# New states of eight streams from doubled rows: two products instead of three, no mask, and the weighting of the doubled rows behind that of the plain rows

## The chip, the cores and the metric

The kernel runs on one core of one Trainium2 chip. The metric is the device time of one execution in microseconds; the number that counts is the median over several runs. The engines are named as the profile names them: PE (TensorE; PEld is its weight load), DVE (VectorE), ACT (ScalarE), POOL (GpSimd) and SP (SyncE, which only issues DMAs here).

## What is computed

One layer of a streaming encoder for 256 prompt rows and, beside them, 16 new rows for each of 8 running streams: 384 rows in all. The layer is a projection, a pooling branch, a state space (SSD) branch, gates, an output product, and an MLP. The change lies in the SSD branch, at the end of this step of the reference:

```python
def step(h, inp):
    xc, dtc, Bc, Cc = inp
    cum = jnp.cumsum(dtc * A, axis=1)
    ...
    y = jnp.einsum('btsgr,bsgrp->btgrp', cb[..., None] * decay, xdt)
    y = y + jnp.einsum('btgn,bgrpn->btgrp', Cc, h) * jnp.exp(cum)[..., None]
    last = cum[:, -1]
    w_end = jnp.exp(last[:, None] - cum)
    h = h * jnp.exp(last)[..., None, None] + jnp.einsum('bsgn,bsgr,bsgrp->bgrpn', Bc, w_end, xdt)
    return h, y
```

The sum over `s` in the last line runs over the 16 rows of one stream for each of the 8 streams `b`: the state that a stream hands on is its old one, decayed, plus a product of the rows `B` with the rows `x`, weighted by `w_end` and `dt`. There are 8 groups `g`, each with 8 heads of 64 channels, and 128 state columns `n`. All of it is fp32.

## The kernel before

**Products.** PE has no fast fp32 product, so the kernel splits each operand into a high part (a cast to the type fp32r, on ACT) and a low part (the operand less its high part, on DVE) and adds three products: high by high, high by low, low by high. For the weights this is `wsplit` (L70 the cast `wh`, L71 the subtraction `wl`), and `mm3` (L101, L102, L103) issues the three; only L103 reads `wl`. A weight matrix comes in half units of 512 KB: a half is fetched by SP's queue, split by ACT and DVE, and read by 24 matmuls. Three halves lie in SBUF at once.

**The SSD stage** runs from about 425 to 1165 us. Its loop goes over the 8 groups. A group projects ten units: x, B, x, C, x, x, all six with a convolution (`cbuf`, `cstate`, `cacc`, `xs`), and four of z (`zproj`, each of two halves). A group's heads form two pairs, `D.p[0]` and `D.p[1]`. Between the projections stand "lumps", short stretches of matmuls that need what the other engines have prepared:

- the middle of a group (behind its fifth unit): for the pair `p[1]` of the group before, the prompt's state (`t_pp`), its outputs (`t_yT`, `t_Y`) and the streams' new states (`t_su`); and for this group's `p[0]` the contribution of the old states (`t_yi`);
- the end of a group: the same for this group's `p[0]`, with `t_yi` of `p[1]`. The last group's `p[1]` follows behind the loop.

**The streams' new states.** `t_su` (L803 on) stands 16 times in the program. It uses PE as four row tiles of 32 rows. The 128 stream rows (16 for each of 8 streams) lie on the 128 partitions, so that one row tile `q` holds the rows of two streams, `2q` and `2q+1`. To get two sums out of one tile, the rows `B` stand twice in `Bm`, once with the second stream's rows put to zero and once with the first's (a multiplication by a mask from `vec`, on ACT, L728). For each of the two and each tile three products are added, as above: 2 × 3 × 4 = 24 matmuls. Four `hs` adds on DVE (L818) then put them onto the decayed states, two streams each, and a DMA stores these.

**What is prepared for it.** `turned` (L622) turns a 128x384 tile of x or B to rows: DVE transposes in blocks (`xb`, L627), POOL stores the blocks to a scratch in DRAM with four DMAs (L632) and fetches them in the right place (L638) as three blocks of 128 rows: two of the prompt, the third the stream rows. `xside` (L758) multiplies the rows by the weights in `tok` on DVE, into `xdt` for the outputs and into `xT` in place for the states. `hside` (L769) splits `xT` into `xhl` on ACT and DVE. `bside` (L721) does so for B and makes `Bm`.

**The order around it.** The kernel is written in one order and a scheduler sets each engine's own; `behind` holds an instruction behind another, `later` and `dve_later` behind the last split of a weight half. Each engine works in its order: an instruction that waits holds all that is behind it. In the middle of a group, `xside` and `hside` of `p[0]` follow on DVE and ACT right behind the lump, together with the convolution of the sixth unit and the splits of the z weights; at the start of a group `p[1]` of the group before is prepared.

## Time and profile before

| | |
|---|---|
| median of 3 runs | 2642.29 us (2642.28 to 2642.95) |
| the profiled execution | 2643.02 us |
| its span | 2641.2 us |
| mean granted clock of PE | 0.999 |
| POOL, share of the span | 9% |
| PE instructions in the profile | 16317 |
| `hs` adds (DVE, L818) | 64, of 0.673 to 0.680 us |
| split `wh_z` (ACT, L70) / `wl_z` (DVE, L71), mean | 1.04 / 1.22 us |

How to read it: the span is that of the profiled execution. "Busy" is the time in which an engine worked. A row of a timeline gives the start in us from the span's start, the duration, the engine, the line of the kernel, the operation, output and inputs, shapes and count, and in square brackets how long the engine stood idle before it and what ended that. A row with "x2" joins neighbours of one kind. On DVE and ACT an instruction's record begins some 0.07 to 0.15 us before the one ahead of it ends, so that starts give the pitch better than durations. In a row of the view by tile the three numbers are the shortest, median and longest duration in ns, then the first and the last start in us.

### The profile page before, as it was taken

The page shows a single profiled execution, that of the slowest core. Times are in us where ns is not written, and L with a number is a line of the kernel's source. Part 1 is how long each engine was busy: PE and PEld are TensorE (multiplying, and loading weights), DVE is VectorE, ACT ScalarE, POOL GpSimd, SP SyncE. Part 2 cuts the span into 40 slices and gives each one's busy share as a digit, 9 for nine tenths or more (in the row PEclk, how much of TensorE's full clock was granted, in tenths as well). Part 3 has the DMA queues.
Part 4 walks back from the last instruction along what each step waited for, and adds up shares of the span by engine and source line. Part 5 has one row for each costly group of instructions (what it writes and reads, how often), then busy time and mean ns, then how long its engine had stood idle before and what let it go on. Part 6 is the DMA issues. An engine that isn't in the chain of part 4 may idle for free.

```text
span 2641.2 us, 40716 instructions
## 1 busy us (share of the span) xinstructions
PE 2631.5 (100%) x16317; PEld 2530.6 (96%) x16317; DVE 1544.6 (58%) x2192; ACT 1161.5 (44%) x1781; POOL 242.4 (9%) x382
## 2 busy tenths in 40 slices
PE   9999999999999999999999999999999999999998
PEld 9999999999999999999999989999999999989897
DVE  6685335788888888867444336534444444444446
ACT  6443324657565656545333336433333333323233
POOL 0000002123222322211000000000000000000000
PEclk9999999999999999999999999999999999999999
DMA  7444446566676666657555544444444444444443
GB/s 274 148 135 154 148 147 222 190 202 227 211 233 201 219 225 230 220 189 261 163 166 160 196 148 132 144 136 136 136 136 136 136 136 135 136 134 136 136 135 131
DMA packets 130318, 451.50 MB, mean 171 GB/s; under 512 B 17936, under 2 KB 24912, under 8 KB 125136
## 3 DMA queue, kind: packets, MB, share of 16 engines
q1 hardware_dynamic: 103552, 361.44, 42.1%
q0 software_dynamic: 19520, 72.64, 7.8%
q10 hardware_dynamic: 7056, 14.81, 1.9%
q8 instruction: 128, 2.10, 0.3%
q14 instruction: 62, 0.51, 0.1%
HBM read 404.49 MB, written 44.34 MB: 170 GB/s over the span
## 4 chain that ended last, share of the span: by engine, by line
PE 99%; ACT 0%; DVE 0%; DMA 0%; DVEq 0%; issue 0%
PE pj_up L101 6%; PE pj_up L103 6%; PE pj_up L102 6%; PE wd L156 6%; PE wd L154 6%; PE wd L155 6%; PE pj_x L101 5%; PE pj_x L102 5%; PE pj_x L103 5%; PE pj_z L103 3%; PE pj_z L101 3%; PE pj_sp L103 3%; PE pj_sp L102 3%; PE pj_sp L101 3%; PE pj_z L102 3%; PE pj_gb L101 2%
## 5 line engine op out<-in xcount | busy, mean ns | idle before, releaser
L101 PE MATMUL pj_up<-x1h,wh_up 128*128 128x384 f32 (+1 forms) x1024 | 333.7, 326 | 0.0
L102 PE MATMUL pj_up<-x1l,wh_up 128*128 128x384 f32 (+1 forms) x1024 | 333.4, 326 | 0.0
L103 PE MATMUL pj_up<-x1h,wl_up 128*128 128x384 f32 (+1 forms) x1024 | 333.4, 326 | 0.0
L71 DVE TENSOR_TENSOR wl_wd<-w_wd,wh_wd 128x1024 fp32r<-128x1024 f32 x126 | 154.3, 1225 | 240.5 <-ACT wh_wd L70 240.5
L154 PE MATMUL wd<-wh_wd,hh 128*128 128x512 f32 x756 | 286.5, 379 | 0.0
L155 PE MATMUL wd<-wl_wd,hh 128*128 128x512 f32 x756 | 286.5, 379 | 0.0
L156 PE MATMUL wd<-wh_wd,hl 128*128 128x512 f32 x756 | 286.5, 379 | 0.0
L70 ACT ACTIVATE wh_wd<-w_wd 128x1024 fp32r<-128x1024 f32 x126 | 133.1, 1057 | 321.8 <-PE wd L156 261.4
L70 ACT ACTIVATE wh_up<-w_up 128x1024 fp32r<-128x1024 f32 x126 | 133.1, 1057 | 292.2 <-PE pj_up L102 231.8
L71 DVE TENSOR_TENSOR wl_up<-w_up,wh_up 128x1024 fp32r<-128x1024 f32 x126 | 154.3, 1225 | 178.3 <-ACT wh_up L70 178.2
L101 PE MATMUL pj_x<-xgh,wh_x 128*128 128x384 f32 x768 | 251.9, 328 | 0.0
L102 PE MATMUL pj_x<-xgl,wh_x 128*128 128x384 f32 x768 | 250.4, 326 | 0.0
L103 PE MATMUL pj_x<-xgh,wl_x 128*128 128x384 f32 x768 | 250.4, 326 | 0.0
L102 PEld LDWEIGHTS pj_up<-x1l,wh_up 128*128 128x128 f32 x1024 | 193.6, 189 | 0.2
L101 PEld LDWEIGHTS pj_up<-x1h,wh_up 128*128 128x128 f32 x1024 | 193.6, 189 | 0.2
L103 PEld LDWEIGHTS pj_up<-x1h,wl_up 128*128 128x128 f32 x1024 | 193.6, 189 | 0.0
L103 PE MATMUL pj_z<-xgh,wl_z 128*128 128x384 f32 x512 | 167.3, 327 | 0.0
L101 PE MATMUL pj_z<-xgh,wh_z 128*128 128x384 f32 x512 | 166.9, 326 | 0.0
L102 PE MATMUL pj_z<-xgl,wh_z 128*128 128x384 f32 x512 | 166.9, 326 | 0.0
L101 PE MATMUL pj_sp<-abh,wh_sp 128*128 128x384 f32 x512 | 166.9, 326 | 0.0
L102 PE MATMUL pj_sp<-abl,wh_sp 128*128 128x384 f32 x512 | 166.9, 326 | 0.0
L103 PE MATMUL pj_sp<-abh,wl_sp 128*128 128x384 f32 x512 | 166.9, 326 | 0.0
(334 smaller groups left out, 6183.5 us busy)
## 6 DMA issues: line engine op xcount, KB each, us to landing
w_up<-w_up SPq DMA_DIRECT2D x128, 512.0 KB, 3.5
w_wd<-w_down SPq DMA_DIRECT2D x128, 512.0 KB, 3.5
w_x<-w_in SPq DMA_DIRECT2D x96, 512.0 KB, 4.1
w_z<-w_in SPq DMA_DIRECT2D x64, 512.0 KB, 4.2
w_sp<-w_ssd SPq DMA_DIRECT2D x64, 512.0 KB, 3.5
w_ga<-w_ga SPq DMA_DIRECT2D x32, 512.0 KB, 3.5
w_pp<-w_pp SPq DMA_DIRECT2D x32, 512.0 KB, 3.4
hs<-ssm POOLq DMA_DIRECT2D x16, 1024.0 KB, 8.0
```

The costliest lines, as they stand in the source:

```text
L70: cut[0] = s.activation(h, w, AF.Copy)
L71: cut[1] = v.tensor_tensor(l, w, h.bitcast(F32), ALU.subtract)
L101: te.matmul(out, wh, xh, start=first, stop=False, **how)
L102: te.matmul(out, wh, xl, start=False, stop=False, **how)
L103: return te.matmul(out, wl, xh, start=False, stop=last, **how)
L154: te.matmul(out, mh, vh, start=k == 0 and b != held, stop=False, skip_group_check=b == held)
L155: te.matmul(out, mh, vl, start=False, stop=False, skip_group_check=b == held)
L156: last[0] = te.matmul(out, ml, vh, start=False, stop=k == nk - 1, skip_group_check=b == held)
```

## The change

The two streams of a row tile are told apart by position and no longer by a mask. Besides the plain rows, each turned tile is fetched a second time with every stream row twice: `doubled` lets partition 2t and partition 2t+1 hold the same row `t` of the 64 rows of half `l` (streams 0 to 3, and 4 to 7). A row tile of 32 partitions then holds the 16 rows of one stream, each twice. On the even partitions of `xd` stands the high part with a minus, on the odd ones the low part; `Bd` is B times −1 on the even and +1 on the odd partitions, once its high part and once its low part. One product over 32 partitions so adds (−high)(−high B) and (low)(high B) in one go, and a second does the same with the low part of B: two products for each half `l` and tile `q`, that is 2 × 2 × 4 = 16 matmuls in place of 24. The tile `su[q]` now belongs to the streams `q` and `q + 4`, so the `hs` adds take those.

What goes: `Bm` and its two ACT casts a group, the third block of `xhl`, `Bhl`, `Bt` and of the product on `xT`. What comes: for each turned tile two more POOL DMAs of 64 KB, at the stage's start a scratch store and two loads for `tokd` (the weights of the doubled rows); for each pair a product `xD` on DVE, a cast `xd` on ACT and a subtraction `xd` on DVE; for each group a cast `Bd` on ACT and a subtraction `Bd` on DVE. The two parity columns of `vec` change their values. The product on `xD` is held behind the last product of `xside`, the cast `xd` behind the cast of `xhl`.

```diff
@@ -210,6 +210,7 @@
     ma_scr = [dram.tile([P, T], F32, name=f"ma_scr{i}") for i in range(KD)]
     gb_scr = [dram.tile([P, T], F32, name=f"gb_scr{i}") for i in range(KD)]
     t_scr = [dram.tile([T, P], F32, name=f"t_scr{i}") for i in range(40)]
+    d_scr = dram.tile([P, NH], F32, name="d_scr")
     cum_scr = dram.tile([NH, T], F32, name="cum_scr")
     dec_scr = dram.tile([NH, NB], F32, name="dec_scr")
 
@@ -619,7 +620,15 @@
         def conv(ui, c, tag, nb, hook=None):
             return taps(conv_in(ui, c, hook), c, tag, nb)
 
-        def turned(src, i, o):
+        def doubled(o, src):
+            for q in range(2):
+                gp.dma_start(o[q::2], src.rearrange("(l t) n -> t l n", l=2))
+
+        tokd = pd.tile([P, 2, NH], F32, name="tokd", bufs=1)
+        gp.dma_start(d_scr, tok[:, 8])
+        doubled(tokd, d_scr)
+
+        def turned(src, i, o, od):
             xb, scr = [], t_scr[i]
 
             def turn():
@@ -635,13 +644,20 @@
                     )
 
             wait = [lambda: None] if i < 32 else []
-            steps.append(wait + [turn, spread, lambda: gp.dma_start(o, scr.rearrange("(b t) n -> t b n", b=3))])
+            nb = o.shape[1]
+
+            def fetch():
+                gp.dma_start(o, scr[: nb * P].rearrange("(b t) n -> t b n", b=nb))
+                doubled(od, scr[TP:])
+
+            steps.append(wait + [turn, spread, fetch])
 
         def xturned(D, g, j):
             S = D.p[j // 2]
             if j % 2 == 0:
                 S.xT = pd.tile([P, 2, 3, P], F32, tag="xT", name=f"xT{S.nm}", bufs=1)
-            turned(D.xs[j], g * 4 + j, S.xT[:, j % 2])
+                S.xD = pd.tile([P, 2, 2, P], F32, tag="xD", name=f"xD{S.nm}", bufs=1)
+            turned(D.xs[j], g * 4 + j, S.xT[:, j % 2], S.xD[:, :, j % 2])
 
         def lump(fn):
             with behind(last[0]):
@@ -719,17 +735,15 @@
             return i
 
         def bside(D):
-            D.Bhl = pd.tile([P, 2, 3, P], F32R, tag="Bhl", name=f"Bhl{D.g}", bufs=1)
+            D.Bhl = pd.tile([P, 2, 2, P], F32R, tag="Bhl", name=f"Bhl{D.g}", bufs=1)
+            D.Bd = pd.tile([P, 2, 2, P], F32R, tag="Bd", name=f"Bd{D.g}", bufs=1)
+            sign = vec[:, V_PAR + 1 : V_PAR + 2]
             with dve_later():
                 s.activation(D.Bhl[:, 0], D.Bt, AF.Copy)
                 v.tensor_tensor(D.Bhl[:, 1], D.Bt, D.Bhl[:, 0].bitcast(F32), ALU.subtract)
-            D.Bm = pd.tile([P, 2, 2, P], F32R, tag="Bm", name=f"Bm{D.g}", bufs=1)
-            for h in range(2):
-                s.activation(
-                    D.Bm[:, h],
-                    D.Bhl[:, :, 2, :].bitcast(F32),
-                    AF.Copy,
-                    scale=vec[:, V_PAR + h : V_PAR + h + 1],
+                s.activation(D.Bd[:, 0], D.BD, AF.Copy, scale=sign)
+                v.scalar_tensor_tensor(
+                    out=D.Bd[:, 1], in0=D.BD, scalar=sign, in1=D.Bd[:, 0].bitcast(F32), op0=ALU.mult, op1=ALU.subtract
                 )
 
         def cside(D):
@@ -758,18 +772,34 @@
             S.xdt = pd.tile([P, 2, 3, P], F32, tag="xdt", name=f"xdt{S.nm}", bufs=1)
             for q in range(2):
                 tv = S.xT[:, q].rearrange("p b (h q) -> p b h q", h=2)
-                for o, i in ((S.xdt, 3), (S.xT, 6)):
-                    v.tensor_tensor(
-                        o[:, q].rearrange("p b (h q) -> p b h q", h=2),
-                        tv,
-                        tok[:, i : i + 3, S.h0 + q * 2 : S.h0 + q * 2 + 2].unsqueeze(3).to_broadcast([P, 3, 2, 64]),
+                for o, i, nb in ((S.xdt, 3, 3), (S.xT, 6, 2)):
+                    done = v.tensor_tensor(
+                        o[:, q, :nb].rearrange("p b (h q) -> p b h q", h=2),
+                        tv[:, :nb],
+                        tok[:, i : i + nb, S.h0 + q * 2 : S.h0 + q * 2 + 2].unsqueeze(3).to_broadcast([P, nb, 2, 64]),
                         ALU.mult,
                     )
+            xD = S.xD.rearrange("p l j (h q) -> p l (j h) q", h=2)
+            with behind(done):
+                v.tensor_tensor(
+                    xD, xD, tokd[:, :, S.h0 : S.h0 + 4].unsqueeze(3).to_broadcast([P, 2, 4, 64]), ALU.mult
+                )
 
         def hside(S):
-            S.xhl = pd.tile([P, 2, 2, 3, P], F32R, tag="xhl", name=f"xhl{S.nm}", bufs=1)
-            S.split = s.activation(S.xhl[:, 0], S.xT, AF.Copy)
-            v.tensor_tensor(S.xhl[:, 1], S.xT, S.xhl[:, 0].bitcast(F32), ALU.subtract)
+            S.xhl = pd.tile([P, 2, 2, 2, P], F32R, tag="xhl", name=f"xhl{S.nm}", bufs=1)
+            S.split = s.activation(S.xhl[:, 0], S.xT[:, :, :2], AF.Copy)
+            v.tensor_tensor(S.xhl[:, 1], S.xT[:, :, :2], S.xhl[:, 0].bitcast(F32), ALU.subtract)
+            S.xd = pd.tile([P, 2, 2, P], F32R, tag="xd", name=f"xd{S.nm}", bufs=1)
+            with behind(S.split):
+                s.activation(S.xd, S.xD, AF.Copy)
+            v.scalar_tensor_tensor(
+                out=S.xd,
+                in0=S.xD,
+                scalar=vec[:, V_PAR : V_PAR + 1],
+                in1=S.xd.bitcast(F32),
+                op0=ALU.mult,
+                op1=ALU.subtract,
+            )
 
         def eside(S, q):
             if q == 0:
@@ -802,19 +832,19 @@
         def state(S):
             def t_su():
                 su = [sstile(f"su{S.nm}_{q}") for q in range(4)]
-                for h in range(2):
-                    for n, (bl, xl) in enumerate(((0, 0), (0, 1), (1, 0))):
+                for l in range(2):
+                    for part in range(2):
                         for q in range(4):
                             t = slice(q * 32, q * 32 + 32)
                             i = te.matmul(
-                                pairs(su[q][:, h * 256 : h * 256 + 256]),
-                                S.D.Bm[t, h, bl, :],
-                                S.xhl[t, xl, :, 2, :].rearrange("p j n -> p n j"),
-                                start=n == 0,
-                                stop=n == 2,
+                                pairs(su[q][:, l * 256 : l * 256 + 256]),
+                                S.D.Bd[t, part, l],
+                                S.xd[t, l].rearrange("p j n -> p n j"),
+                                start=part == 0,
+                                stop=part == 1,
                             )
                 for q in range(4):
-                    hr = S.hs[:, 2 * q : 2 * q + 2].rearrange("p h (a n) -> p h a n", a=2)
+                    hr = S.hs[:, q::4].rearrange("p h (a n) -> p h a n", a=2)
                     v.tensor_tensor(hr, hr, su[q].rearrange("p (h n a) -> p h a n", h=2, a=2), ALU.add)
                 return i
 
@@ -929,8 +959,9 @@
                 xturned(D, g, 0)
                 eside(prev.p[1], 0)
             D.BT = conv(u0 + 1, 32 + g, "BT", 2, None if g else first_behind)
-            D.Bt = pd.tile([P, 3, P], F32, tag="Bt", name=f"Bt{g}", bufs=1)
-            turned(D.BT, 32 + g, D.Bt)
+            D.Bt = pd.tile([P, 2, P], F32, tag="Bt", name=f"Bt{g}", bufs=1)
+            D.BD = pd.tile([P, 2, P], F32, tag="BD", name=f"BD{g}", bufs=1)
+            turned(D.BT, 32 + g, D.Bt, D.BD)
             if g:
                 eside(prev.p[1], 1)
                 expside(prev.p[1])
@@ -1458,8 +1489,8 @@
     vec[:, V_DSK:V_DTB] = chan(np.repeat(a["d_skip"][0], 64))
     vec[:NH, V_DTB] = a["dt_bias"][0]
     vec[:NH, V_ALOG] = a["a_log"][0]
-    for h in range(2):
-        vec[:, V_PAR + h] = (np.arange(P) // TS_) % 2 == h
+    vec[:, V_PAR] = np.arange(P) % 2
+    vec[:, V_PAR + 1] = 2.0 * (np.arange(P) % 2) - 1.0
     d = {
         "cst": _consts(np),
         "vec": vec,
```

The change also lets the scheduler come to another order. DVE in the middle of one group (the others but the first read alike), behind the lump: `hs` are the old pair's states, `xdt`, `xT`, `xD` the new pair's rows, `wl_z` the low halves of the z weights. Before:

```order
L762 TENSOR_TENSOR xdt_0_7615<-xT_0_7174,tok 128x384 x2
L818 TENSOR_TENSOR hs_1_6843<-hs_1_6843,su_1_0_7562 128x512
...
L762 TENSOR_TENSOR xT_0_7174<-xT_0_7174,tok 128x384 x2
L627 STREAM_TRANSPOSE xb_7685<-xs_7613 128x384
L772 TENSOR_TENSOR xhl_0_7620<-xT_0_7174,xhl_0_7620 128x768
L71 TENSOR_TENSOR wl_z_0_1_7658<-w_z_0_1_7655,wh_z_0_1_7657 128x1024
L593 TENSOR_TENSOR cbuf_4141<-pj_x_7624,rstd 128x12x16 x2
L71 TENSOR_TENSOR wl_z_1_0_7712<-w_z_1_0_7709,wh_z_1_0_7711 128x1024
```

With the change, from the same point on:

```order
L848 TENSOR_TENSOR hs_1_6875<-hs_1_6875,su_1_0_7598 128x2x256
...
L776 TENSOR_TENSOR xdt_0_7643<-xT_0_7202,tok 128x384 x2
L776 TENSOR_TENSOR xT_0_7202<-xT_0_7202,tok 128x256 x2
L784 TENSOR_TENSOR xD_0_7203<-xD_0_7203,tokd 128x512
L636 STREAM_TRANSPOSE xb_7718<-xs_7641 128x384
L791 TENSOR_TENSOR xhl_0_7649<-xT_0_7202,xhl_0_7649 128x512
L795 SCALAR_TENSOR_TENSOR xd_0_7652<-xD_0_7203,vec,xd_0_7652 128x512
L71 TENSOR_TENSOR wl_z_0_1_7691<-w_z_0_1_7688,wh_z_0_1_7690 128x1024
L594 TENSOR_TENSOR cbuf_4142<-pj_x_7657,rstd 128x12x16 x2
L613 SCALAR_TENSOR_TENSOR cacc_7725<-cbuf_4142,vec,cacc_7725 128x384 x2
L71 TENSOR_TENSOR wl_z_1_0_7745<-w_z_1_0_7742,wh_z_1_0_7744 128x1024
```

The four `hs` adds have moved ahead of `xdt`, two instructions on `xD` and `xd` stand between, and two `cacc` steps have moved ahead of the second `wl_z` of the piece (the third half of the z weights).

ACT at the same place, from the cast of `xhl` on. Before:

```order
L771 ACTIVATE xhl_0_7620<-xT_0_7174 128x768
L70 ACTIVATE wh_z_0_1_7657<-w_z_0_1_7655 128x1024
L789 ACT_TABLE_LOAD
L789 ACTIVATE E_0_7699<-E_0_7699 128x2048
L70 ACTIVATE wh_z_1_0_7711<-w_z_1_0_7709 128x1024
L601 COPY cbuf_4141<-cbuf_4141 128x15x3
L602 COPY cstate<-cbuf_4141 128x27
L610 ACTIVATE cacc_7692<-cbuf_4141,vec 128x384
L661 DMA cbc_1_1_7790<-cum_scr 128x768
L197 ACTIVATE nh_g_7936<-ssum_7084 128x384
L70 ACTIVATE wh_z_1_1_7745<-w_z_1_1_7743 128x1024
```

With the change:

```order
L790 ACTIVATE xhl_0_7649<-xT_0_7202 128x512
L794 ACTIVATE xd_0_7652<-xD_0_7203 128x512
L70 ACTIVATE wh_z_0_1_7690<-w_z_0_1_7688 128x1024
L819 ACT_TABLE_LOAD
L819 ACTIVATE E_0_7732<-E_0_7732 128x2048
L602 COPY cbuf_4142<-cbuf_4142 128x15x3
L603 COPY cstate<-cbuf_4142 128x27
L611 ACTIVATE cacc_7725<-cbuf_4142,vec 128x384
L70 ACTIVATE wh_z_1_0_7744<-w_z_1_0_7742 128x1024
L677 DMA cbc_1_1_7825<-cum_scr 128x768
L70 ACTIVATE wh_z_1_1_7778<-w_z_1_1_7776 128x1024
```

The cast `xd` has come behind that of `xhl`; the split of the third z half now follows the three convolution steps instead of leading them, and `nh_g` has left the piece.

POOL between two turned tiles of a group and the lump. Before:

```order
L632 DMA t_scr_141<-xb_5373 32x12x32 x4
L638 DMA xT_0_5124<-t_scr_141 128x3x128
L847 TENSOR_TENSOR ssum_5034<-ssum_5034,ysq_2_5550 128x384
L847 TENSOR_TENSOR ssum_5034<-ssum_5034,ysq_3_5555 128x384
L822 DMA new_ssm_s<-hs_1_4821 128x2048
```

With the change:

```order
L641 DMA t_scr_141<-xb_5397 32x12x32 x4
L650 DMA xT_0_5142<-t_scr_141 128x3x128
L625 DMA xD_0_5143<-t_scr_141 64x2x128 x2
L877 TENSOR_TENSOR ssum_5048<-ssum_5048,ysq_2_5568 128x384
L877 TENSOR_TENSOR ssum_5048<-ssum_5048,ysq_3_5573 128x384
L852 DMA new_ssm_s<-hs_1_4843 128x2048
```

Each fetch is followed by the two doubled loads; nothing else changes place on POOL here.

## The prediction

> **What bounds the kernel now.** I read the page first, for the engine that sets the end, then the view of the waits of TensorE.
>
> ```profile
> PE 2631.5 (100%) x16317; PEld 2530.6 (96%) x16317; DVE 1544.6 (58%) x2192; ACT 1161.5 (44%) x1781; POOL 242.4 (9%) x382
> PE 99%; ACT 0%; DVE 0%; DMA 0%; DVEq 0%; issue 0%
> PE pj_p L317 <- ACT xgh L277: 0.3, 1, 0.3
> ```
>
> PE (TensorE) is busy for 2631.5 of 2641.2 us and holds 99% of the chain that ended last; its view of waits names only a start-up wait beside the row shown. So a matmul that is gone is time gained, and work on VectorE (DVE), ScalarE (ACT) or POOL costs only where it makes PE pause. The average says nothing about where that is. The change lies in the scan stage, where the chain in order of time shows the edited lump, and the view by tile its number:
>
> ```profile
> 500.54 0.67 PE py L711 x6
> 504.20 0.87 PE su L809 x24
> ...
> L809 PEld LDWEIGHTS su<-xhl,Bm x384: 181/187/187, 504.1 to 1161.1; 32*128 32x128 f32 x192
> ```
>
> 384 matmuls at 24 a lump are 16 lumps, from 504 to 1161 us. Four row tiles of K=32 run beside each other, so that 24 small matmuls are six passes, and each lump stands on the chain with 0.87 us.
>
> Next the timeline of DVE, ACT, POOL and PE in one lump's wake, where DVE has the most added work: group 3's new states, read by the `hs` adds, and the four z projections behind them.
>
> ```profile
> 730.61 1.83 DVE L762 TENSOR_TENSOR xdt<-xT,tok 128x384 f32<-128x384 f32 x2
> 732.36 2.47 DVE L818 TENSOR_TENSOR hs<-hs,su 128x512 f32<-128x512 f32 x4
> 734.75 1.01 DVE L762 TENSOR_TENSOR xT<-xT,tok 128x384 f32<-128x384 f32 x2
> 735.69 0.56 DVE L627 STREAM_TRANSPOSE xb<-xs 128x384 f32<-128x384 f32 x1
> 736.72 0.96 DVE L772 TENSOR_TENSOR xhl<-xT,xhl 128x768 fp32r<-128x768 f32 x1 [0.47 <-ACT xhl L771]
> 737.68 1.23 DVE L71 TENSOR_TENSOR wl_z<-w_z,wh_z 128x1024 fp32r<-128x1024 f32 x1
> 741.86 1.23 DVE L71 TENSOR_TENSOR wl_z<-w_z,wh_z 128x1024 fp32r<-128x1024 f32 x1 [2.42 <-ACT wh_z L70]
> 743.00 1.27 DVE L612 SCALAR_TENSOR_TENSOR cacc<-cbuf,vec,cacc 128x384 f32<-128x384 f32 x2
> 744.18 0.55 DVE L198 TENSOR_TENSOR nl_g<-ssum,nh_g 128x384 fp32r<-128x384 f32 x1
> ...
> 735.85 0.84 ACT L771 ACTIVATE xhl<-xT 128x768 fp32r<-128x768 f32 x1 [1.59 <-PE pj_x L103]
> 736.60 1.05 ACT L70 ACTIVATE wh_z<-w_z 128x1024 fp32r<-128x1024 f32 x1
> 738.96 1.92 ACT L789 ACTIVATE E<-E 128x2048 f32<-128x2048 f32 x1
> 740.79 1.03 ACT L70 ACTIVATE wh_z<-w_z 128x1024 fp32r<-128x1024 f32 x1
> 741.73 0.22 ACT L601 COPY cbuf<-cbuf 128x45 f32<-128x45 f32 x1
> 742.52 0.51 ACT L197 ACTIVATE nh_g<-ssum 128x384 fp32r<-128x384 f32 x1
> ...
> 730.92 1.10 POOL L847 TENSOR_TENSOR ssum<-ssum,ysq 128x384 f32<-128x384 f32 x1 [1.18 <-ACT ysq L846]
> ...
> 742.84 0.33 PE L102 MATMUL pj_z<-xgl,wh_z 128*128 128x384 f32 x1
> 743.13 0.43 PE L103 MATMUL pj_z<-xgh,wl_z 128*128 128x384 f32 x1
> ```
>
> The reader is to see a chain that hangs by a thread. PE issues a matmul each 0.163 us and should start the first one that reads the low half `wl_z` at 743.00; that split ends at 741.86 + 1.23 = 743.09, and the matmul begins at 743.13 and is 0.10 longer. This is a pause of about 0.23 us that the list of waits does not name. It is the third half of the z weights (the second reads the split of 737.68). The same pair, end of the split and first matmul on it, in the groups 2, 4, 5 and 7:
>
> ```profile
> 652.72 1.22 DVE L71 TENSOR_TENSOR wl_z<-w_z,wh_z 128x1024 fp32r<-128x1024 f32 x1 [2.42 <-ACT wh_z L70]
> 654.29 0.33 PE L103 MATMUL pj_z<-xgh,wl_z 128*128 128x384 f32 x1
> ...
> 830.18 1.23 DVE L71 TENSOR_TENSOR wl_z<-w_z,wh_z 128x1024 fp32r<-128x1024 f32 x1 [2.42 <-ACT wh_z L70]
> 832.14 0.33 PE L103 MATMUL pj_z<-xgh,wl_z 128*128 128x384 f32 x1
> ...
> 919.40 1.23 DVE L71 TENSOR_TENSOR wl_z<-w_z,wh_z 128x1024 fp32r<-128x1024 f32 x1 [2.41 <-ACT wh_z L70]
> 920.80 0.33 PE L103 MATMUL pj_z<-xgh,wl_z 128*128 128x384 f32 x1
> ...
> 1096.67 1.23 DVE L71 TENSOR_TENSOR wl_z<-w_z,wh_z 128x1024 fp32r<-128x1024 f32 x1 [2.42 <-ACT wh_z L70]
> 1098.35 0.33 PE L103 MATMUL pj_z<-xgh,wl_z 128*128 128x384 f32 x1
> ```
>
> The room is 0.35, 0.73, 0.17 and 0.45 us; the other groups have more and are counted at nothing.
>
> **The change part by part: PE.** A lump falls from 24 to 16 matmuls, six passes to four. A pass of 256 columns takes 0.67 / 6 = 0.112 us by the chain's `py` row, so two are 0.224 us a lump and 16 × 0.224 = 3.58 us in all. If the fixed part of the 0.87 us fell in proportion too, it would be 0.87 / 3 × 16 = 4.64. I take 3.58: 0.87 is 0.20 more than six passes, and that rest looks like a change of tile shape, which stays.
>
> **DVE and ACT up to the third z half.** The product on `xT` shrinks by a third and `xhl` from 768 to 512 columns; a product on `xD` (128x512) and a subtraction `xd` come to DVE, a cast `xd` to ACT. The adds also move ahead of the two `xdt` products. The view by tile, and a place where the adds ran under a POOL instruction already (group 3's end):
>
> ```profile
> L762 DVE TENSOR_TENSOR xdt<-xT,tok x32: 542/549/1367, 462.5 to 1134.8; 128x384 f32<-128x384 f32 x32
> ...
> 773.66 1.76 POOL L847 TENSOR_TENSOR ssum<-ssum,ysq 128x384 f32<-128x384 f32 x1 [2.10 <-ACT ysq L846]
> ...
> 774.47 2.47 DVE L818 TENSOR_TENSOR hs<-hs,su 128x512 f32<-128x512 f32 x4
> ```
>
> One `xdt` of each pair takes 1.36 instead of 0.55 us, while POOL's `ssum` at 730.92 runs; the four adds take 2.47 whether POOL is silent (732.36) or in the middle of its product (774.47). In the changed order the adds stand beside POOL and `xdt` behind it, so 1.36 − 0.55 = 0.81 us are saved. The Trainium skill ("SBUF — State Buffer", "Who interferes with whom") says it as a rule: a DVE instruction with two SBUF inputs contends with a GpSimd one that reads SBUF, one with at most one SBUF input does not; the adds read one input from PSUM, and the trace agrees (1.36 against 0.55, 2.47 against 2.47). By the rule the 0.81 are gained; if instead whatever DVE ran there paid, they would not be, and the sum below would rise by what the second rival says.
>
> The replay, from 730.61. Adds 2.39 (732.36 to 734.75), two `xdt` 0.94 (the two `xT` of the same size: 734.75 to 735.69), two smaller `xT` 0.67: the end is 734.61 instead of 735.69. Then `xD` 0.60 (a quarter of 2.39, same size) and `xb` 0.49 end at 735.70. ACT meanwhile casts `xhl` (0.5 us by 0.75 × 512/768, the step from 735.85 to 736.60) and `xd` (0.5), the latter held until `xD` is ready at 735.3, and starts its split at about 735.9 instead of 736.60. DVE subtracts `xhl` (0.64) and `xd` (0.53 to 0.59 × 512/384, so 0.7 to 0.8), and the second half's `wl_z` starts near 737.1, 0.6 early. On ACT the table load and `E` follow, also 0.7 early, but now `cbuf`, `cstate` and `cacc` stand ahead of the third split: 741.73 to 742.52 is 0.79, so that split starts 0.1 late, at 740.9. On DVE two `cacc` steps (743.00 to 744.18: 1.1 to 1.2) stand ahead of `wl_z` too; they can start when ACT's `cacc` ends near 740.95 and end at 742.1. The third `wl_z` is thus 0.23 us later than 741.86, with everything behind the wait (`wl_z`, then PE) in turn.
>
> PE arrives 0.224 us earlier, since the lump before is shorter, so the room must hold 0.23 + 0.22 = 0.45. Group 3, which pauses already, pays 0.45; group 2 lacks 0.10, group 5 0.28, each with 0.10 for a matmul that restarts longer (0.43 against 0.33): 0.20 and 0.38. Group 7 stands at its limit: 0.05. Together 1.08 us. Bounds for this shift: at best nothing is later and today's pauses vanish; at worst the 0.81 is not gained and both new DVE operations cost in proportion to their slowest rows (`xd` 1.27 / 2 × 512/384 = 0.85, `xD` 0.55 × 512/384 = 0.73, together 0.28 more): 0.23 + 0.81 + 0.28 = 1.32. I take 0.23, since the two gains rest on rows of the same instructions.
>
> **The fifth z half.** Its first low product starts late today too:
>
> ```profile
> 751.18 0.43 PE L103 MATMUL pj_z<-xgh,wl_z 128*128 128x384 f32 x1
> ```
>
> The split ahead of it no longer stands behind `nl_g` and the third `cacc` (together about 1 us by the rows at 744.18 and 743.00), and of two `Bm` casts one `Bd` cast is left, while a subtraction for `Bd` costs 0.4 (0.53 to 0.59 × 256/384), a quarter of it saved on the smaller `Bhl`. So the fifth split comes up to 1 us earlier, and the pause at 751.18 goes, with the same one in group 5: 2 × 0.23 = −0.46. If this is wrong, nothing is lost but the 0.46.
>
> **POOL.** Each of the 40 turned tiles gets two more DMAs, and there are three at the stage's start: 83.
>
> ```profile
> 721.07 0.75 POOL L638 DMA_DIRECT2D xT<-t_scr  x1 [2.06 <-DMA t_scr<-xb]
> ...
> DMA to landing us min/median/max: 2.7/3.6/8.4
> ...
> L632 POOL DMA_DIRECT2D t_scr<-xb x160: 616/618/661, 438.7 to 1106.5; - x160
> ```
>
> At 0.62 to 0.75 us an issue, a fetch is 1.2 to 1.5 us longer on an engine that is 9% busy; 83 are at most 63 us. The row at 721.07 is the last fetch ahead of group 3's products. Its two doubled loads would be issued by 721.07 + 3 × 0.75 = 723.3, and land by 726.9 at the median of 3.6 us, by 731.7 at the worst of 8.4; DVE reads `xD` at 734.6 in the replay. I put nothing down. The cover is POOL's idleness: where it fails, what POOL issues next goes 1.5 us later each time. The Trainium skill ("SBUF — State Buffer", "SBUF: two separate sides") speaks against this part: DMAs issued from GpSimd can starve for descriptors while DVE runs an operation in a two-port mode. The issues of `t_scr` spread only from 616 to 661 ns over the stage, so the trace shows none of it, though it shows no landing of such small doubled loads; by the rule the price would be a later landing, the third rival.
>
> **Sum.** −3.58 + 1.08 − 0.46 = −2.96 us, so 2643.02 − 2.96 = 2640.1 in the profiled execution, which lies 0.73 above the median of 2642.29: **2639.4** for the median.
>
> **The rivals.** First, the whole saving and more: the third split is not late, all pauses (three of 0.23) go, and the lump falls in proportion: −3.58 − 0.69 = −4.3, or −4.64 − 0.69 = −5.3, that is 2638.0 to 2637.0. For it: the replay is tight by 0.1 us on each engine. Against: two engines both now have work ahead of that split.
>
> Second, slower: the third z half's split decides. If the 0.81 is not gained and the new operations are at their upper rows, the shift is 1.32 and the room must hold 1.54: group 2 pays 1.29, 3 1.54, 4 0.91, 5 1.47, 7 1.19, each with its 0.10 where it runs freely today: 6.4. −3.58 + 6.4 − 0.46 = +2.4, so 2644.7. It outweighs the saving from a shift of about 0.87 us on, and passes +5.3 us near 1.9. For it: today's rows there have no slack in groups 3 and 5. Against: the measured 2.47 under POOL.
>
> Third, the doubled loads land late or hold POOL's queue up: DVE then waits at `xD` with all splits behind it. One us in each of 16 pairs beyond the room would cost, with a third of them hidden or none, 10 to 16 us, less the 2.96 of the sum: 2649 to 2655. It decides from a landing of some 11 us on (734.6 − 723.3). Against: the worst landing of 8.4 us.
>
> Fourth, the change does not do what it says: a pass is not the unit (16 matmuls with longer fixed parts), so the lump stays near 0.87 and time is within 1 us of before: 2642.5 or, with the 1.08, 2643.
>
> **How the numbers follow.** Forecast 0.54; whole saving 0.12; z split 0.20; late loads 0.08; no saving 0.06. One measurement of this kernel tells 0.2%, 5.3 us, from no change. Below 2637.0 lies only the end of the first rival (0.03). Above 2647.6 lie most of the third (0.07) and the far end of the second, with shifts the rows do not show (0.08). So faster 0.03, slower 0.15, the same 0.82. The range: from 2637.9, the first rival's nearer end, to 2646.5, which holds the second up to a shift of 1.6; left out are some 0.05 below and 0.15 above. The forecast's own range is 2638.0 to 2641.
>
> **What would show it.** Right: `su` lumps of 16 matmuls at about 0.65 us in the chain; `xdt` at 0.55 in every mid-group; adds still 0.68; the third `wl_z` 0.2 us later against the lump before; pauses of up to half a us in groups 2, 3 and 5; no pause at the fifth half. Wrong: an `xdt` or an add of 1.3 us, a pause at group 4's third half, DVE idle before `xD` with a DMA named, POOL rows above 0.8 us, or lumps still at 0.87.

## The result and the profile after

The changed kernel takes 2638.42 us (median of 22 runs, 2637.18 to 2639.55), the kernel before 2642.39 us in the same sessions (22 runs, 2641.07 to 2644.39): a ratio of 0.9984, with a 95% interval from 0.9977 to 0.9991. That is 4.0 us less, within 2.4 to 6.1. Forecast were 2.9 us less. The execution of the changed kernel that was profiled took 2639.55 us, the longest of the 22.

The page of the changed kernel, the same lines as were shown of before:

```profile
span 2637.6 us, 40653 instructions
...
PE 2627.4 (100%) x16189; PEld 2527.1 (96%) x16189; DVE 1550.9 (59%) x2232; ACT 1163.6 (44%) x1789; POOL 287.6 (11%) x465
```

PE is still the bound, with 128 instructions fewer; DVE has 6 us more work and POOL 45 us more, and neither shows in the span. The chain in order of time of the changed kernel, at the first lump and the last (start, duration, work):

```profile
501.28 0.67 PE py L727 x6
504.94 0.65 PE su L839 x16
...
1157.23 0.65 PE su L839 x16
```

and the same two lumps of the kernel before:

```profile
504.20 0.87 PE su L809 x24
...
1160.60 0.87 PE su L809 x24
```

A lump fell from 0.87 to 0.65 us, as the price of a pass said. From the first lump's start to the last one's it was 1160.60 − 504.20 = 656.40 us and is 1157.23 − 504.94 = 652.29. This "stage time" leaves out what varies from run to run at the program's start, and it is the measure of most experiments below. 4.11 us went; 15 shorter lumps account for 15 × 0.224 = 3.36, and 0.75 are left. These are the three pauses of the z halves in the kernel before (0.24 each at 743, 751 and 929 us) and a delay of 0.05 at 662, which are all gone. DVE, POOL and PE of the changed kernel in group 3, timeline rows that answer to those shown of before (rows left out are marked):

```profile
728.62 2.47 DVE L848 TENSOR_TENSOR hs<-hs,su 128x512 f32<-128x512 f32 x4
731.01 1.01 DVE L776 TENSOR_TENSOR xdt<-xT,tok 128x384 f32<-128x384 f32 x2
731.95 0.75 DVE L776 TENSOR_TENSOR xT<-xT,tok 128x256 f32<-128x256 f32 x2
732.62 0.68 DVE L784 TENSOR_TENSOR xD<-xD,tokd 128x512 f32<-128x512 f32 x1
...
734.28 0.73 DVE L795 SCALAR_TENSOR_TENSOR xd<-xD,vec,xd 128x512 fp32r<-128x512 f32 x1
734.99 1.22 DVE L71 TENSOR_TENSOR wl_z<-w_z,wh_z 128x1024 fp32r<-128x1024 f32 x1
...
740.20 1.22 DVE L71 TENSOR_TENSOR wl_z<-w_z,wh_z 128x1024 fp32r<-128x1024 f32 x1
...
728.93 1.00 POOL L877 TENSOR_TENSOR ssum<-ssum,ysq 128x384 f32<-128x384 f32 x1 [1.18 <-ACT ysq L876]
...
742.35 0.33 PE L103 MATMUL pj_z<-xgh,wl_z 128*128 128x384 f32 x1
```

The two `xdt` products now follow POOL's and take 1.01 together instead of 1.83, and the adds are no slower beside it. The third half's `wl_z` ends at 741.42, and the first matmul that needs it starts at 742.35 when PE wants it: a room of 0.93 us where before there was a pause. The room (start of that matmul, as PE's pitch gives it, less the end of the split) is the same in groups 1 to 7, and that is the surprise:

| room at the third z half, us | group 1 | 2 | 3 | 4 | 5 | 6 | 7 |
|---|---|---|---|---|---|---|---|
| before | 1.49 | 0.36 | −0.08 | 0.74 | 0.17 | 1.49 | 0.46 |
| change | 0.94 | 0.94 | 0.94 | 0.93 | 0.94 | 0.94 | 0.94 |

One new pause stands at the stage's start, in the timelines of ACT and PE of the changed kernel:

```profile
434.13 0.44 ACT L601 COPY cbuf<-cstate 128x24 f32<-128x24 f32 x3 [8.90 <-DMA cstate<-state_conv]
...
436.00 0.33 PE L102 MATMUL pj_x<-xgl,wh_x 128*128 128x384 f32 x1
436.84 0.43 PE L103 MATMUL pj_x<-xgh,wl_x 128*128 128x384 f32 x1 [0.51 <-DVE wl_x L71]
```

The load of the convolution's state, `cstate`, holds ACT and the splits behind it. The matmul should have started at 436.16; with its longer duration it costs 0.78 us. So in the two profiles the spans differ by 3.6: −3.59 (16 lumps) − 0.75 + 0.78, and 0.04 from the program's first 232 us.

### The profile page after: what moved, and what is told of

Read it like the earlier page. It is cut to its first block, busy times and chain, and to the rows that moved or that the text cites. A ratio compares the mean times of both kernels' runs of the same rounds, so it can differ in the third digit from the quotient of the medians.

```text
span 2637.6 us, 40653 instructions
## 1 busy us (share of the span) xinstructions
PE 2627.4 (100%) x16189; PEld 2527.1 (96%) x16189; DVE 1550.9 (59%) x2232; ACT 1163.6 (44%) x1789; POOL 287.6 (11%) x465
## 3 DMA queue, kind: packets, MB, share of 16 engines
q8 instruction: 127, 2.08, 0.3%
## 4 chain that ended last, share of the span: by engine, by line
PE 99%; DMA 1%; issue 0%; ACT 0%; DVE 0%; DVEq 0%; POOLq 0%; ACTq 0%
PE pj_up L101 6%; PE pj_up L103 6%; PE pj_up L102 6%; PE wd L156 6%; PE wd L155 6%; PE wd L154 6%; PE pj_x L101 5%; PE pj_x L103 5%; PE pj_x L102 5%; PE pj_sp L102 3%; PE pj_z L102 3%; PE pj_sp L103 3%; PE pj_sp L101 3%; PE pj_z L103 3%; PE pj_z L101 3%; PE pj_gb L101 2%
```

## The experiments

Two questions were open: what makes the room even (the early reading was the order of ACT at a group's start), and whether the pause at 436 us belongs to the change. The spans of single profiles differ by up to 2 us because the program's first 232 us take from 230.2 to 232.2 in them; so the stage time and the room are compared.

**e1: three products again.** In `t_su` (`start` and `stop` follow the new count; the source is otherwise the same):

```diff
-                    for part in range(2):
+                    for n, part in enumerate((0, 1, 1)):
```

> The changed kernel, but with three products per half and tile in the streams' new states (the product with the low part of B is added twice, so the new states are not the reference's): 24 matmuls a lump again, all else as in the change. Theory (passes): PE gets back two passes of 0.112 us in each of 16 lumps, so lumps of 0.87 us and a span of 2637.6 + 3.6 = 2641.2 us, with no pause at a z half, since PE only comes later. Rival (the saving came from the order of the other engines, not from the passes): a span within 1 us of 2637.6.

The lumps are 0.87 us again. From the first lump to the fifteenth it is 621.07 us against 617.49, 3.58 more: 14 × 0.224 = 3.14, and about 0.45 for pauses at the third z half of groups 1 (0.31) and 7 (0.15), where none was expected. They are there because the eight matmuls more made the scheduler choose another order as well: `xdt` stands ahead of the adds again, one of each mid-group pair takes 1.36 us, and the room in the other groups is only 0.34 to 0.41. And the span is 2644.3, 6.7 more. The rest lies in one place, found in PE's view of waits of e1, with what ACT waited for ahead of it:

```profile
PE pj_gb L101 <- DVE zs L1009: 2.3, 1, 2.3
...
1118.20 1.06 ACT L70 ACTIVATE wh_gb<-w_gb 128x1024 fp32r<-128x1024 f32 x1 [3.42 <-DMA w_gb<-w_gb]
```

DVE has the same order here as in the kernel before and in the change: behind the split of `w_gb` come ten norm steps, with another split between them, and then the product `zs` that PE waits for. What is late is the weight half `w_gb`: it landed 7.2 us after its issue (before: 5.9, change: 5.4), and it was issued 1.2 us later against the lump than in the kernel before. The windows of e1 around it (length, busy time of PE, PEld, DVE, ACT, POOL with counts, then PE's granted clock, DMA share, GB/s) show a second price:

```profile
1120.00:1125.00 5.00, 5.00 (x93) 3.98 (x96) 4.79 (x9) 1.93 (x2) 0.00 (x0) 1.00 0.35 111
1125.00:1130.00 5.00, 2.74 (x30) 2.58 (x23) 4.93 (x10) 0.53 (x1) 1.58 (x3) 0.88 0.43 139
1130.00:1135.00 5.00, 5.00 (x25) 5.00 (x25) 5.00 (x10) 2.36 (x4) 2.01 (x3) 0.78 0.57 171
```

After 2.3 us of idle the granted clock fell to 0.88 and 0.78, and for 3 us the matmuls came every 0.32 instead of 0.163 us. So this run shows the price of a pass only up to the fifteenth lump.

**e2: one product.** The low part of B is left out of the new states:

```diff
-                    for part in range(2):
+                    for n, part in enumerate((0,)):
```

> The changed kernel with one product only (the low part of B is left out of the new states): 8 matmuls a lump. Theory (a pass costs 0.112 us and the rest of a lump is fixed): lumps of 0.65 - 0.22 = 0.43 us, span 2637.6 - 3.6 = 2634.0 us. Rival (a lump's cost is in proportion to its matmuls): 0.33 us a lump, span 2632.4.

The stage time is 648.95 us, 652.29 − 648.95 = 3.34 less for 15 lumps, 0.223 each; the chain of e2 has

```profile
503.47 0.42 PE su L839 x8
```

so 0.87, 0.65 and 0.42 for six, four and two passes: 0.112 a pass and 0.20 fixed. The rival (cost in proportion) falls. No z half pauses here, though the scheduler changed the order again, so this run has the price alone. The span of 2632.6 lies between the two forecasts because this run began earlier and had 0.08 of the pause at the stage's start.

**e3: the kernel before with the group's start in the new order.** The start of a group differs on ACT as well: the changed kernel splits the next weight half ahead of the exponential `E`, the kernel before behind it. One line brings this into the kernel before:

```diff
-                expside(prev.p[1])
+                with behind(prev.p[1].split):
+                    expside(prev.p[1])
```

> The kernel before, with one change of order: at a group's start the exponential of the old pair is held behind the cast of xhl on ACT, so that the split of the next weight half goes first, as in the changed kernel. Products and DVE's order in the middle of a group stay. Theory (start of the group): the splits no longer run late, DVE reaches the lump about 2 us earlier in groups 2 to 5 and 7, the room at the third z half is 1.4 to 1.5 us in all groups from 1 on, the three pauses (743, 751, 929 us) are gone: span about 2641.2 - 0.75 = 2640.4. Rival (the adds ahead of xdt did it): the three pauses stay, rooms as before (0.35, -0.08, 0.73, 0.17, 1.49, 0.45), span 2641.2.

The theory's signs all came: rooms of 1.49 to 1.55 in groups 1 to 7, no pause, a stage time of 655.65, exactly 0.75 less than 656.40, with the lumps still at 0.87. (The span of 2639.4 has 1.1 us of the early start in it.) So neither the adds nor the products of the change are needed to take the pauses away.

**e5: the change with the old start.** The reverse: in the changed kernel the split of that weight half is held behind the exponential, which with the products that it needs is written earlier in the group.

```diff
-        cut[0] = s.activation(h, w, AF.Copy)
+        with behind(hold.get(name)):
+            cut[0] = s.activation(h, w, AF.Copy)
...
+                hold[f"x{32 + g}_1"] = expside(prev.p[1])
             b0 = conv_in(u0, g * 4)
```

> The changed kernel with the old order at a group's start: the exponential of the old pair goes on ACT ahead of the split of the next weight half again, as in the kernel before. Products, doubled loads and the order in the middle of a group are those of the change. Theory (the pauses went away because of the start of the group): the splits run late again, DVE comes to the lump 2 us later, and the room at the third z half is that of the kernel before less 0.45 us in each group (about -0.1, -0.5, 0.3, -0.3, 1.0, 0.0 in groups 2 to 7), with pauses in groups 2, 3 and 5: about 1 us more between the first and the last lump than the 652.3 us of the changed kernel. Rival (the order in the middle of the group did it): room stays at 0.94 in every group, no pause, 652.3 us.

The theory fell: the stage time is 652.30 and the room 0.94 in six groups (0.66 in group 1). The order at a group's start can undo the pauses (e3), but e5 has none without it. Something else had to tell e3 and the kernel before apart. It lies in the landings of single weight loads, in the view by tile limited to one load. The kernel before, group 3, then group 6 of the same run, which had a room of 1.49:

```profile
L63 SPq DMA_DIRECT2D w_x<-w_in x1: 328/328/328, 692.8 to 692.8; - x1
DMA to landing us min/median/max: 8.1/8.1/8.1
...
L63 SPq DMA_DIRECT2D w_x<-w_in x1: 328/328/328, 959.7 to 959.7; - x1
DMA to landing us min/median/max: 3.8/3.8/3.8
```

and the load of the old states in those two groups:

```profile
L655 POOL DMA_DIRECT2D hs<-ssm x1: 538/538/538, 692.6 to 692.6; - x1
DMA to landing us min/median/max: 8.3/8.3/8.3
...
L655 POOL DMA_DIRECT2D hs<-ssm x1: 533/533/533, 960.0 to 960.0; - x1
DMA to landing us min/median/max: 5.9/5.9/5.9
```

In group 3 this 1 MB load is issued some 0.1 us ahead of the 512 KB weight half, and both land together at 700.9; in group 6 it goes some 0.3 us behind, and the weight half lands in 3.8. Over the seven groups of the kernel before, the landing of this half orders the rooms without exception:

| group | 1 | 6 | 4 | 7 | 2 | 5 | 3 |
|---|---|---|---|---|---|---|---|
| landing of the half, us | 3.6 | 3.8 | 7.0 | 7.3 | 7.7 | 7.8 | 8.1 |
| room at the third z half, us | 1.49 | 1.49 | 0.74 | 0.46 | 0.36 | 0.17 | −0.08 |

The timeline of ACT in group 3 and the view of `w_x` by tile (515 to 1068 us) of the kernel before show the wait:

```profile
700.91 1.06 ACT L70 ACTIVATE wh_x<-w_x 128x1024 fp32r<-128x1024 f32 x1 [2.24 <-DMA w_x<-w_in]
701.88 0.22 ACT L601 COPY cbuf<-cbuf 128x45 f32<-128x45 f32 x1
702.01 0.21 ACT L602 COPY cstate<-cbuf 128x27 f32<-128x27 f32 x1
702.13 0.63 ACT L610 ACTIVATE cacc<-cbuf,vec 128x384 f32<-128x384 f32 x1
...
  DMA w_x<-w_in: 8.6, 5
```

ACT waits for this half in five groups, which are the five with a small room, and the three convolution steps behind it, which DVE needs, come late with it. DVE does not make it up: its first `xdt` starts 4.50 us behind the lump's start in group 3, and 2.95 in groups 1 and 6.

**e9: only the state load moved.** In the kernel before, the `hs` load of `p[0]` is held on POOL behind the four stores of the group's first turned tile. No other engine's order changes.

```diff
-            gp.dma_start(S.hs, io["ssm"][S.qd])
+            with behind(spreads[0] if S.g and S.jp == 0 else None):
+                gp.dma_start(S.hs, io["ssm"][S.qd])
```

> The kernel before; only the POOL load of p[0]'s old states (hs, 1 MB) in groups 1 to 7 is held behind the four stores of the group's first turned tile, so it goes out about 20 us behind the lump's start instead of 11 us. The orders of ACT, DVE, PE and SP are the same as before. Theory (collision: the fourth weight half's transfer starts at the same time as this load and lands 4 us late, and that lateness stays in the splits up to the z halves): that transfer lands 3.5 to 4.5 us after its issue in every group, the room at the third z half is about 1.49 us in all groups 1 to 7, no pause at z halves, 656.40 - 0.75 = 655.65 us from the first to the last lump. Rival (the order of ACT at the group's start or the adds decide it): rooms and pauses stay irregular, 656.4 us.

The load goes out 27 to 28 us behind the lump's start (20 were expected), the weight half lands in 3.5 to 4.5 us in every group, and ACT waits for none. In group 3 of e9 the third split and its first matmul are

```profile
740.16 1.23 DVE L71 TENSOR_TENSOR wl_z<-w_z,wh_z 128x1024 fp32r<-128x1024 f32 x1 [2.41 <-ACT wh_z L70]
...
742.88 0.33 PE L103 MATMUL pj_z<-xgh,wl_z 128*128 128x384 f32 x1
```

a room of 1.49, and all groups have 1.49 to 1.55. There is no pause, and the stage time is 655.65 us. The collision of two loads on the DMA engines, 40 us ahead of the place where PE waits, made the pauses.

By the trace, e3 worked because it frees the weight half's place 2.5 us earlier: the state load comes 4 us behind, and the half lands at 13.8 to 14.6 us from the lump's start in groups 2 to 7, in place of 18.5 to 19.3 in the late groups of before. The changed kernel has such an early start too: the weight half goes out 8.7 to 8.9 us behind the lump's start (before: 11.3 to 11.5 in groups 2 to 7) and lands in 3.4 to 4.1 us, and the state load follows 1.6 us or more behind. That this is what made its rooms even is read from the traces; no run shows it.

In e5 the two loads meet again (landings of 6.4 to 7.9 us in five groups) and the room still holds. But e5 has an order on ACT that neither kernel has, here in group 7, where the half landed in 7.9 us:

```profile
1050.11 0.24 ACT L604 COPY cbuf<-cbuf 128x45 f32<-128x45 f32 x1
1050.25 0.21 ACT L605 COPY cstate<-cbuf 128x27 f32<-128x27 f32 x1
1050.38 0.65 ACT L613 ACTIVATE cacc<-cbuf,vec 128x384 f32<-128x384 f32 x1
1051.86 1.06 ACT L72 ACTIVATE wh_x<-w_x 128x1024 fp32r<-128x1024 f32 x1 [0.83 <-DMA w_x<-w_in]
```

The convolution steps stand ahead of the split and do not wait for it. In the change the split stands ahead of them, as in the kernel before. So e5 does not tell whether the changed kernel would bear a late half.

**e6: `xdt` ahead of the adds, in the changed kernel.** `xside` is cut in two, and the adds are emitted behind its first part and held there:

```diff
-                xside(S)
+                xside1(S)
+                if g:
+                    with behind(S.weighed):
+                        prev.p[1].add()
+                xside2(S)
```

> The changed kernel with the xdt products ahead of the hs adds in the middle of a group, as before the change; the rest as in the change. Theory (POOL slows a product with two inputs from SBUF): one xdt of each mid-group pair takes 1.36 us again, the adds stay at 2.47 for four, the room at the third z half falls from 0.94 to about 0.13 us (0.81 less), and since it stays above zero the time does not move: 652.3 us from the first to the last lump. Rival (whatever runs beside POOL pays, or the products are slowed by something else): xdt stays at 0.55, room at 0.94.

The view by tile of e6 has the slow product again, which the changed kernel (545/550/558) has not:

```profile
L773 DVE TENSOR_TENSOR xdt<-xT,tok x32: 545/551/1367, 461.4 to 1129.9; 128x384 f32<-128x384 f32 x32
```

The rooms are 0.10 to 0.15 us in six groups, 0.8 less, as forecast; in group 5 no `xdt` is slow and the room is 0.94. The time did move a little: the stage takes 652.77, 0.48 more, in five delays of up to 0.05 and one of 0.2 behind the last group, so a room of 0.1 us is not quite room. In this run the order of adds and `xdt` is worth 0.8 us of room and half a us of stage time; without it the change would stand at the edge.

**e10: the adds ahead of `xdt`, in the kernel before.** `added` is the last `hs` add of the old pair; the split of the products (`hside`) is held with them:

```diff
-            with nullcontext() if g else behind(S.ready):
+            with behind(prev.p[1].added) if g else behind(S.ready):
                 xside(S)
                 hside(S)
```

> The kernel before; only the xdt and xT products in the middle of a group are held behind the hs adds. Theory (POOL slows xdt by 0.81 us, and this is a second, separate part): no xdt of 1.36 us in a mid-group, and the room at the third z half is 0.8 us more than the same landing of the fourth weight half gave before (0.7 us at a landing of 8 us, 2.3 at one of 3.6). Rooms stay irregular, since the collision stays; the pause at group 3's third half goes. Rival: rooms as before.

No `xdt` above 0.55 us is left, and the rooms are 1.55 to 1.60 at landings of 8.2 to 8.5 us, where −0.1 stood before: 1.6 more, not 0.8, and 3.2 in groups 1 to 3. The pauses at z halves are gone, yet the stage time is 656.78, 0.38 more than before: with the state load still beside the weight half, the lateness comes out elsewhere. An x half pauses for 0.24 us at 802.5, and the mid-group lumps of groups 4 to 7 are 0.1 to 0.3 us longer, in the chain of e10 for group 4

```profile
814.79 1.19 PE su L809 x24
```

instead of 0.87. So 0.8 us of the 1.6 were not expected. ACT's timeline of e10 in group 3 shows where they come from:

```profile
732.27 1.05 ACT L70 ACTIVATE wh_z<-w_z 128x1024 fp32r<-128x1024 f32 x1
733.21 0.84 ACT L771 ACTIVATE xhl<-xT 128x768 fp32r<-128x768 f32 x1
...
737.19 1.04 ACT L70 ACTIVATE wh_z<-w_z 128x1024 fp32r<-128x1024 f32 x1
```

The split `wh_z` of the second half now fills the time in which ACT stood idle ahead of the cast `xhl` (1.59 us in the kernel before). The third split so comes 3.98 us behind that cast and no longer 4.94 (735.85 to 740.79 there). This is a second effect of the edit; the slowed product accounts for the other 0.8.

**e4 and e8: the pause at the stage's start.** There the load of `cstate` lands late and holds ACT, and with it a split. In e4 the two small `tokd` loads of the change, which stood right behind it, go out 20 us later, behind the plain fetch `f` of the first turned tile; e8 has this and holds the first `hs` load as well:

```diff
         gp.dma_start(d_scr, tok[:, 8])
-        doubled(tokd, d_scr)
...
                 doubled(od, scr[TP:])
+                if i == 0:
+                    with behind(f):
+                        doubled(tokd, d_scr)
...
-            gp.dma_start(S.hs, io["ssm"][S.qd])
+            with behind(spreads[0] if S.g == 0 and S.jp == 0 else None):
+                gp.dma_start(S.hs, io["ssm"][S.qd])
```

> The changed kernel with the two small loads of the doubled rows' weights (tokd) held on POOL behind the first doubled tile, 20 us later, out of the way of the load of cstate at the stage's start. Theory (they delay cstate): cstate lands near 431.4 instead of 434.1 us, the pause of 0.78 us at 436.8 us on PE is gone, span 2637.6 - 0.8 = 2636.8, median about 2637.6. Rival (cstate is late because its space comes free late, or by chance): the landing stays near 434 and the pause too, 2637.6.

> As e4_tokd_later (the loads of tokd out of the way), and also the first two loads of old states (hs, 1 MB each) held behind the first stores of turned rows, some 15 us later, so that cstate and the next weight half have the DMA engines to themselves at the stage's start. Theory (cstate is late because it shares the DMA engines with what is issued within 2 us of it): cstate lands 4 to 6 us after its issue instead of 7.9, no pause on PE near 436 us, span about 0.45 us shorter than e4's for the same start, median about 2637.8. Rival (its landing hangs on its own many rows, or on chance): 7 to 8 us again, the pause stays.

In e4 `cstate` landed after 7.9 us all the same, and PE paused 0.45 us: the theory that `tokd` is the cause fell. In e8 it landed after 5.8 us and the pause was gone, as its theory said, but 0.16 us were lost at a z half of group 0; and e11 below has 5.9 with nothing moved, so e8 does not tell the theory from chance. Both took about as long as the change: e4 2638.22 us (11 runs, ratio to before 0.998, 0.9971 to 0.9989), e8 2638.57 us (ratio 0.9988, 0.9979 to 0.9997).

**e11: the changed kernel once more.**

> The changed kernel once more, for a second profile. Theory (the pause of 0.78 us at 436.8 us hangs on how cstate's load falls against the weight half issued beside it, by chance of the execution): room at the third z half again 0.94 us in every group, 652.29 us from the first to the last lump, and another pause near 436 us, between none and 1 us, longer the later cstate lands. Rival (it is a fixed cost of the change): 0.78 us again.

The rooms are 0.93 to 0.99, the stage time 652.30, and `cstate` landed after 5.9 us; there is no pause near 436 us. So the 0.78 us are not a fixed cost of the change. Over the profiles of kernels with the `tokd` loads in their place, `cstate` landed after 5.4, 5.9, 6.1 and 6.7 us without a pause (e5, e11, e7, e6), after 7.4 with one of 0.08 (e2), and after 7.9 and 8.2 with 0.78 and 0.93 (the change, e1). In four profiles of the kernel before and its variants (before, e3, e9, e10) it was 5.7, 6.6, 6.6 and 6.9, with no pause. Whether the change makes late landings likelier can't be told from so few.

**e7: the doubled loads twice.**

```diff
                 doubled(od, scr[TP:])
+                doubled(od, scr[TP:])
```

> The changed kernel with every doubled load issued twice into the same place (80 DMAs of 64 KB more on POOL's queue). Theory (POOL's idle time covers them): no DVE wait at xD, room at the third z half within 0.2 us of 0.94, 652.3 us from the first to the last lump, POOL busy for some 50 us more. Rival (the loads hold up POOL's queue or the weights' transfers): DVE idle ahead of xD or xdt, or late weight halves, and 0.5 us or more from the first to the last lump.

Mixed; POOL was busy for 49 us more. In groups 1 to 7 all but group 4 have rooms of 0.78 to 1.66, and the stage time is 652.86, 0.57 more, from one pause in group 4. But group 0 loses 2.7 us ahead of the first lump. DVE of e7 there, then POOL and DVE in group 4:

```profile
467.95 0.69 DVE L785 TENSOR_TENSOR xD<-xD,tokd 128x512 f32<-128x512 f32 x1 [2.04 <-issue]
...
817.66 1.22 POOL L625 DMA_DIRECT2D xD<-t_scr  x2 [2.51 <-DMA xD<-t_scr]
818.90 2.31 POOL L878 TENSOR_TENSOR ssum<-ssum,ysq 128x384 f32<-128x384 f32 x2
...
818.45 3.17 DVE L777 TENSOR_TENSOR xdt<-xT,tok 128x384 f32<-128x384 f32 x2
```

In group 0 the second pair of loads waited for the first to land, `xD` was complete at 467.88, and DVE stood idle for 2.0 us with the z splits behind it. In the changed kernel the same loads land at 465.66 and the product starts at 467.2: 1.5 us of cover, in this one group. In group 4 the wait of the second pair held POOL's queue, so that `ssum` came beside the two `xdt`, which took 3.17 us together instead of 1.01: the rival's way (POOL's queue held up) and the slowed product at once. In the changed kernel `ssum` ends some 1.1 us ahead of `xdt` there.

## Why the prediction was right, and where its reasons failed

- **The passes: right.** 3.58 us forecast, 16 × 0.224 = 3.59 found; e2 gives the same price, and the fixed 0.20 us stays, so the upper bound of 4.64 is out.
- **The adds beside POOL: right.** 0.81 us of room was forecast, e6 takes 0.8 us of room away. The Trainium skill ("SBUF — State Buffer", "Who interferes with whom") had it so, and the rows of e6 (up to 1.37 us beside POOL) and of the changed kernel (0.55) bear it out.
- **The third z half: the step that failed.** The prediction put down +1.08 us, from a shift of 0.45 us set against the rooms of the kernel before, group by group. The shift itself was about right: in groups 1 and 6, where nothing had been late, the room went from 1.49 to 0.94, 0.55 less. Wrong was to carry over the small rooms of groups 2 to 5 and 7. They were not a property of the chain at that place but the trace of a weight half that had landed late beside the state load 40 us earlier (e9), and in the change that half goes out and lands early. The replay began at 730.61, where DVE was already 1.55 us later behind the lump than in groups 1 and 6; it should have asked why two of seven groups had 0.75 to 1.6 us more room than the others. In place of +1.08 stands −0.24, the pause of group 3 that went.
- **The fifth z half: right.** −0.46 was put down; the two pauses of 0.24 there went, with the delay of 0.05 in group 2. The forecast reason is in the traces too: in groups 1 and 6 the room at the fifth half rose from 1.25 to 2.08 though PE came 0.22 earlier, so that split comes 1.05 us earlier, as forecast. But it was not the only reason, since in e3 and e9 the same pauses went without it.
- **POOL's queue: right in the sum, with little to spare.** The doubled loads cost nothing that was seen and landed after 3.6 us in the median and 7.9 at most, as put down (3.6 and 8.4). But in group 0 the cover is 1.5 us, not several, and e7 shows a price that the prediction did not name: loads that hold POOL's queue push `ssum` beside `xdt`.
- **Not foreseen:** the pause at the stage's start, 0.78 and 0 us in the two profiles of the change and up to 0.93 in its variants (e1).

In place of −3.58 + 1.08 − 0.46 = −2.96 stand −3.59 − 0.75 = −4.34, and 0 to 0.9 back at the stage's start. The measured −4.0 lies between, though its interval (−6.1 to −2.4) holds the forecast of −2.9 too. That the time fell within the forecast's range is in part luck: the wrong +1.08 and the pause that nobody foresaw push the same way. Without that pause it is the first rival's time (−4.3), for another reason than that rival gave: the third split was not merely on time, what had made it late was gone. The second rival (2644.7) needed small rooms and a slowed `xdt`; neither was there.

## What to carry to other kernels

Where like groups of a loop have unlike rooms at the same instruction, look upstream first, as here: for a transfer whose landing orders them, before you set a shift against the room of each. When two large loads are issued within a few tenths of a us of each other, the one that a busy engine needs should have a clear head start; moving a state load that nobody waits for yet (e9) took away every pause at the z halves, and the stage time showed no cost. And when an edit changes the number of matmuls or holds one instruction, compare the orders of all engines first: e1, e5 and e10 each changed more than was meant. An engine with little busy time is not cover by itself: count the room of the tightest group.

## What the runs showed of the hardware

The weight half of 512 KB lands 3.5 to 4.5 us after its issue when the 1 MB state load is out of its way (e9), and in 7.0 to 8.1 us when that load is issued within 0.15 us of it (five groups of before); both then land at nearly the same time. Issued 0.34 us behind the half, the state load left it at 3.8 us (group 6), and 4 us behind it at 5.0 to 5.7 (e3). After 2.3 us of idle PE in e1 the granted clock was 0.88 and 0.78 in the two windows of 5 us, and the matmuls ran at half their pace for 3 us: together 4.0 us for one late weight half (39.01 us between the last two lumps, against 35.03 before), in one execution. The Trainium skill ("TensorE: Matmul & The Clock Gate", "Part 1: The HAM clock gate (the "warmup" mystery)") knows the half rate, and the spacing of 0.32 against 0.163 us agrees with it. It puts the fall behind an idle stretch of about 3.4 us; here 2.3 us came ahead of it.
